# A hybrid two-layer diffusion step: row sums for 28 adaLN pieces, one SSD matrix a head, and products of zeros in the prologue

## The chip, the cores and the metric

The kernel runs on one core of one Trainium2 chip. The metric is the device time of one execution in microseconds. The engines that matter here are TensorE (PE, matmuls, and PEld, its weight loads), VectorE (DVE), ScalarE (ACT), GpSimd (POOL) and SyncE (SP, which issues nearly all DMAs).

## What is computed

One inference step through two trunk layers of width 1024 for 640 tokens: 128 context tokens, conditioned by `c_ctx`, and 512 latent tokens, conditioned by `c`. Each layer has an adaLN projection, a combined input projection that feeds four mixers (a bidirectional Mamba-2 SSD, an S5, a differential attention and a windowed attention), an output projection, and a squared-ReLU MLP of width 4096. The change touches two of these computations. The first is the adaLN projection, from which the six parts (shift, scale and gate of the norm and of the MLP) come; a part has 1024 outputs for each of the two conditions:

```python
def adaln(cvec, w, b):
    m = jax.nn.silu(cvec) @ w + b                  # w: 1024 x 6144, a matrix a layer
    return jnp.split(m[:, None, :], 6, axis=-1)
...
    sh1, sc1, g1, sh2, sc2, g2 = adaln(cmod, P['w_mod'][l], P['b_mod'][l])
```

The second is the part of the SSD inside a chunk of 128 tokens, for 8 heads of 64 columns, forward and backward:

```python
def ssd_chunked_scan(x, dt, a_log, bm, cm, s0):
...
    lmat = jnp.exp(jnp.where(lower, seg, NEG_INF))
    xdt = xc * dtc[..., None]
    scores = jnp.einsum('bcthn,bcshn->bctsh', cc, bc) * lmat
    y_diag = jnp.einsum('bctsh,bcshp->bcthp', scores, xdt)
...
    y_f, s_f = ssd_chunked_scan(xs, dt[:, :, 0], a_log[0], bm, cm, s0[:, 0])
    y_b, s_b = ssd_chunked_scan(flip(xs), flip(dt[:, :, 1]), a_log[1], flip(bm), flip(cm), s0[:, 1])
    y = y_f + flip(y_b) + d_skip.astype(f32)[:, None] * xs.astype(f32)
```

## The kernel before, in words

**Dense products.** Activations lie with features on partitions and the 640 tokens along the free axis, in two halves of 320. Every dense product splits both operands into a high and a low part: ACT copies the high part out (wh, L212), DVE or POOL subtracts it from the raw weights for the low part (wl, L196), and TensorE does three matmuls for each block of 128 rows: hi x hi (L223), lo activation x hi weights (L224) and hi activation x lo weights (L225). A half of a dense product with 1024 inputs is thus 24 matmuls of 128x320, and it ends in the PSUM tile dn, which has two buffers. An eviction on DVE or ACT frees it.

**The MLP** runs in four quarters. In each, eight products with w_fc1 (their evictions: ACT's ReLU, then DVE's product r at L1746, ACT's copy fh and the low part fl) are followed by eight with w_fc2, whose evictions are the residual adds on DVE (x, L1538, two instructions each, since context and latent tokens have gates of their own).

**adaLN pieces.** A piece is 256 outputs of one part. `adaln` multiplies the two conditions, padded to 32 columns (cpad), with eight blocks of w_mod (L288, eight matmuls in the code, 16 rows of the trace), copies the result to SBUF on ACT (mrow, L293), turns it with two matmuls by sel (L295, 4 rows of the trace), and adds the bias on DVE (mod, L298). Of 48 pieces in a layer, the prologue does parts 0 and 1 of layer 0 (`panel_adaln`, weights in wm); the other 40 come from `adaln_ahead`, with weights in the ring wa, which has eight buffers of 128x512. Of layer 0's other 16, four run in the mixers' stage, eight in the output projection, and the four of part 5 in the MLP. The 24 of layer 1 run in layer 0's MLP, too. There the function `between` is called after every dense product and takes five steps in eight calls out of one list: pieces, then the steps of the S5 build of layer 1 (`s5_build`, which prepares the S5's matrices on DVE, POOL, ACT and, at L633 and L660, TensorE), then pieces again.

**SSD.** For each of five chunks a layer and two groups of four heads: ACT makes the exponentials ee of both directions (tile sseg), POOL multiplies them by the masked scores of the backward direction into mf (L1033), DVE multiplies them in place by those of the forward direction (L1034), and TensorE then does two matmuls a head, one for each direction, with x times dt (sxd, two products on POOL at L1006): L1037 and L1038, 80 of each over the ten chunks of the two layers, each 128x64 and two rows of the trace. The masked scores themselves (scb) come from DVE at L999.

**Prologue.** TensorE's first work are the pieces of parts 0 and 1 in four panels q, whose weights (wm, 1 MB for each part and panel) come by DMA; beside them ACT and DVE square x for the first norm, and TensorE sums the squares into rb.

**What sets the order.** The instructions of each engine run in a fixed order that a scheduler writes down at build time from its own estimates; `tc.high_priority` moves a block ahead in it, and `tc.issue_after` places one behind a given instruction. Semaphores hold an instruction until its inputs and buffers are there.

## Time and profile before

| what | value |
|---|---|
| median of 3 runs | 2989.94 us (2985.88 to 3001.45) |
| the profiled execution: time, span of its trace | 2994.21 us, 2992.4 us |
| busy: PE, DVE, ACT, POOL | 95%, 56%, 39%, 28% of the span |
| mean granted TensorE clock | 0.976 |
| stretches: prologue, mixers of layer 0, output projection and norm, MLP of layer 0 | to 62, to 960, to 1062, to 1605 us |
| mixers of layer 1, MLP of layer 1 | to 2430, from 2515 us |

The page gives the busy time of each engine, the span in slices, the DMA queues, and the chain of work that ended last, followed back from the end. The trace behind it can be asked for groups of instructions by line, for waits (which engine stood still, at which line, and who released it), for windows of time, and for the plain sequence of an engine. A busy time on TensorE is the length of records that lap over each other, since matmuls are pipelined; the start-to-start distance tells what a row holds up.

### The profile page before, as it was taken

How to read it: one execution, taken by the hardware profiler on the slowest of the kernel's cores; microseconds unless marked ns; L12 is line 12 of the kernel's file. 1: busy time of each engine (PE TensorE's matmuls, PEld its weight loads, DVE VectorE, ACT ScalarE, POOL GpSimd, SP SyncE). 2: the span in 40 equal slices, each digit the busy share in tenths (PEclk: the TensorE clock that was granted, in tenths of full speed). 3: DMA queues.
4: the chain of work that ended last, by engine and by line, in shares of the span. 5: the costliest groups of instructions: out<-in, count | busy, mean ns of one | idle time of the engine just before them, and what ended most of it. 6: DMA issues, size and time to landing. Idle time of an engine off the chain costs nothing.

```text
span 2992.4 us, 53739 instructions
## 1 busy us (share of the span) xinstructions
PE 2831.8 (95%) x20782; PEld 2651.5 (89%) x20782; DVE 1686.3 (56%) x3574; ACT 1181.3 (39%) x2692; POOL 832.8 (28%) x823
## 2 busy tenths in 40 slices
PE   7889998999799999999999999989999999999999
PEld 5878988898689888899998989978997999999999
DVE  7859737665543456646235686576665436433333
ACT  4344563253344242323234555424534434332322
POOL 2743106522212222424111220363131131211111
PEclk9989999998899999999999999989999999999999
DMA  6753343234432635434443433432262323222222
GB/s 225 256 174 112 100 136 102 80 99 136 141 100 75 239 103 174 146 114 159 153 144 112 158 100 115 136 92 66 86 198 86 103 89 106 68 75 78 75 75 85
DMA packets 241855, 364.19 MB, mean 122 GB/s; under 512 B 42272, under 2 KB 104480, under 8 KB 241600
## 3 DMA queue, kind: packets, MB, share of 16 engines
q1 hardware_dynamic: 226848, 336.97, 36.0%
q10 hardware_dynamic: 14752, 23.78, 2.2%
q8 instruction: 164, 2.69, 0.4%
q14 instruction: 91, 0.75, 0.1%
HBM read 294.98 MB, written 65.68 MB: 121 GB/s over the span
## 4 chain that ended last, share of the span: by engine, by line
PE 72%; DVE 13%; DMA 4%; issue 3%; ACT 2%; POOL 2%; SPq 0%; DVEq 0%; ACTq 0%; POOLq 0%
PE dn L223 20%; PE dn L224 20%; PE dn L225 20%; DVE wl L196 2%; DMA sseg<-acum 1%; PE mx L288 1%; PE mx L1278 1%; PE pb L1322 1%; PE mx L1407 1%; PE mx L1452 1%; PE mx L1316 1%; DVE B L767 1%; DVE sc L766 1%; PE mx L743 1%; DVE cv L902 1%
## 5 line engine op out<-in xcount | busy, mean ns | idle before, releaser
L196 POOL TENSOR_TENSOR wl<-wr,wh 128x512 fp32r<-128x512 f32 x207 | 287.1, 1387 | 1340.7 <-ACT wh L212 1254.5
L212 ACT CAST wh<-wr 128x512 fp32r<-128x512 f32 (+1 forms) x614 | 377.3, 620 | 600.5 <-PE dn L224 525.1
L196 DVE TENSOR_TENSOR wl<-wr,wh 128x512 fp32r<-128x512 f32 (+1 forms) x407 | 326.4, 805 | 318.1 <-ACT wh L212 306.4
L223 PE MATMUL dn<-hh,wh 128*128 128x320 f32 x1328 | 422.3, 318 | 12.3 <-ACT us L695 3.8
L224 PE MATMUL dn<-hl,wh 128*128 128x320 f32 x1328 | 420.2, 316 | 2.8 <-DVE hl L401 1.5
L225 PE MATMUL dn<-hh,wl 128*128 128x320 f32 x1328 | 418.8, 316 | 1.6 <-DVE wl L196 1.6
L223 PE MATMUL dn<-nh,wh 128*128 128x320 f32 x992 | 311.1, 314 | 6.6 <-DVE r L1746 6.6
L223 PE MATMUL dn<-fh,wh 128*128 128x320 f32 x1008 | 313.6, 311 | 2.9 <-DVE x L1538 2.9
L224 PE MATMUL dn<-nl,wh 128*128 128x320 f32 x992 | 308.5, 311 | 3.9 <-DVE nl L401 1.6
L225 PE MATMUL dn<-fh,wl 128*128 128x320 f32 x1008 | 312.1, 310 | 0.0
L224 PE MATMUL dn<-fl,wh 128*128 128x320 f32 x1008 | 311.8, 309 | 0.0
L225 PE MATMUL dn<-nh,wl 128*128 128x320 f32 x992 | 307.6, 310 | 0.0
L223 PEld LDWEIGHTS dn<-hh,wh 128*128 128x128 f32 x1328 | 253.4, 191 | 19.4 <-ACT us L695 4.1
L223 PE MATMUL dn<-wh,hh 128*128 128x256 f32 (+1 forms) x880 | 259.2, 296 | 8.2 <-DVE dtraw L1207 3.0
L224 PE MATMUL dn<-wl,hh 128*128 128x256 f32 (+1 forms) x880 | 256.8, 293 | 10.5 <-DVE wl L196 8.5
L224 PEld LDWEIGHTS dn<-hl,wh 128*128 128x128 f32 x1328 | 253.3, 191 | 8.3 <-issue 3.2
L225 PEld LDWEIGHTS dn<-hh,wl 128*128 128x128 f32 x1328 | 253.2, 191 | 6.9 <-issue 3.8
L225 PE MATMUL dn<-wh,hl 128*128 128x256 f32 (+1 forms) x880 | 256.0, 292 | 0.0
L1538 DVE SCALAR_TENSOR_TENSOR x<-dn,mod,x 128x192 f32<-128x192 f32 (+2 forms) x240 | 98.0, 436 | 225.2 <-PE dn L225 217.7
L223 PE MATMUL dn<-B,wh 128*128 128x320 f32 x640 | 206.2, 323 | 12.7 <-ACT B L825 3.4
L224 PE MATMUL dn<-B,wh 128*128 128x320 f32 x640 | 202.1, 316 | 0.2 <-DVE B L196 0.2
L225 PE MATMUL dn<-B,wl 128*128 128x320 f32 x640 | 200.4, 313 | 0.0
(399 smaller groups left out, 6505.6 us busy)
## 6 DMA issues: line engine op xcount, KB each, us to landing
wr<-in_w_fc_dram SPq DMA_DIRECT2D x256, 256.0 KB, 2.8
wa<-in_w_mod_dram SPq DMA_DIRECT2D x160, 256.0 KB, 4.5
wr<-in_w_gate_dram SPq DMA_DIRECT2D x128, 256.0 KB, 2.8
wr<-in_w_tok_dram SPq DMA_DIRECT2D x80, 256.0 KB, 2.9
wr<-in_w_branch_dram SPq DMA_DIRECT2D x64, 256.0 KB, 3.0
acc<-gth SPq DMA_DIRECT2D x48, 320.0 KB, 3.1
gold<-acc SPq DMA_DIRECT2D x48, 320.0 KB, 3.7
gate<-gah ACTq DMA_DIRECT2D x70, 160.0 KB, 1.8
```

Of the source, the lines that this page charges most:

```text
L196: engine.tensor_tensor(out=out, in0=full, in1=hi, op=ALU.subtract)
L212: nc.scalar.copy(out=hi, in_=raw)
L223: nc.tensor.matmul(ps, sh, vh, start=first, stop=False)
L224: nc.tensor.matmul(ps, sh, vl, start=False, stop=False)
L225: nc.tensor.matmul(ps, sl, vh, start=False, stop=last)
L288: nc.tensor.matmul(acc[r0:r0 + 32, i * 256:i * 256 + 256], cpad[:, k, :], raw(part, k // 2)[:, c0:c0 + 256], start=(n_ < 4), stop=(n_ >= 4),)
L743: nc.tensor.matmul(xs[:, ri, g * NI:(g + 1) * NI], pm[:, ri, g * 128:(g + 1) * 128], U[:, g0 + g], start=True, stop=True)
L766: nc.vector.tensor_tensor(out=t, in0=v.to_broadcast(shp), in1=x.to_broadcast(shp), op=ALU.mult)
L767: nc.vector.tensor_tensor(out=dst, in0=dst, in1=t, op=ALU.add)
L902: nc.vector.scalar_tensor_tensor(out=cv, in0=xp[:, k:k + 646], scalar=cw[:, f, k:k + 1], in1=cv, op0=ALU.mult, op1=ALU.add)
L1278: nc.tensor.matmul(sc[:, n, c0:c0 + (k1 - k0) * 128], qT[rows[n], g, ct], kT[rows[n], k0:k1].rearrange("p k c -> p (k c)"), start=True, st ...
L1538: nc.vector.scalar_tensor_tensor(out=xs, in0=ps[:, c0:c1], scalar=mods[l][:, part * 8 + f, s:s + 1], in1=xs, op0=ALU.mult, op1=ALU.add)
```

## The change

There are three edits.

**Row sums.** Part 5 of both layers and parts 0 to 4 of layer 1 are no longer computed on TensorE. Of the pieces before, 28 go: the four of part 5 of layer 0 and the 24 of layer 1. In their place `adaln_rows` loads, for each block of 128 outputs, the 128x1024 block of the transposed weights (a new input, w_modt), and lets DVE multiply it with a condition that is the same on all partitions and sum along the row, with the bias as start (`tensor_tensor_reduce`, two for each block, one for each condition; each is two rows in the order, both at L352). The conditions come through DRAM: silu on a new input c_rows in the prologue, stored to c_d, and broadcast to 128 partitions in each MLP (`cond_rows`, 1 MB). 96 row sums run in layer 0's MLP and 16 (its own part 5) in layer 1's. `fill` places one behind each residual add and each product r. The ring wa has three buffers of 128x1024 now, `between` takes one step of the S5 build in every sixth call, and the build's tiles s5u and s5v have one buffer each in the MLP.

**SSD.** The two directions' masked scores are scaled by dt (a column for each row of the matrix, so it can stand on either side of the product) and added before the exponentials come in: ACT's scaled copy and DVE's scalar-tensor-tensor for each head, tile smd. DVE multiplies ee by the sum, and one matmul a head with x itself (L1075) remains. POOL's products mf and sxd for this sum are gone.

**Zeros.** `busy(n)` multiplies a tile of zeros in bf16, 128x128 by 128x128, n times: 80 times at the start, 120 times behind the first panel's adaLN, 40 times behind the second's call.

```diff
-    t1=3, tx=4, tq=6, ty=2, tw=5, td=5, nt=4, wa=8, wr=4, wh=4, wl=4, fh=10,
+    t1=3, tx=4, tq=6, ty=2, tw=5, td=5, nt=4, wa=3, wr=4, wh=4, wl=4, fh=10,
...
+    cr = tmp([128, 16], "cr", bufs=1)
+    sp.dma_start(out=cr, in_=a["c_rows"])
...
+    nc.vector.tensor_tensor(out=cr, in0=cr, in1=crt, op=ALU.mult)
+    c_d = dp.tile([128, 16], F32, name="c_d")
+    sp.dma_start(out=c_d, in_=cr)
...
+                    if n // 2 not in halves:
+                        halves[n // 2] = wa([128, 1024], "wa")
+                        sp.dma_start(out=halves[n // 2], in_=a["w_mod"][part * 4 + q, n // 2])
...
+    def cond_rows():
+
+        cb = big([128, 2, D], "cb")
+        sp.dma_start(out=cb.rearrange("p s k -> p (s k)"), in_=c_d.rearrange("a b -> (a b)").unsqueeze(0).to_broadcast((128, 2 * D)))
+        return cb
+
+    def adaln_rows(l, parts, cb, after=()):
+
+        for part in parts:
+            for f in range(part * 8, part * 8 + 8):
+                with tc.high_priority(offset=AHEAD):
+                    w = wa([128, D], "wa")
+                    sp.dma_start(out=w, in_=a["w_modt"][l * 48 + f - 40])
+                prod = mx().rearrange("p a b -> p (a b)")
+                for s in range(2):
+                    nc.vector.tensor_tensor_reduce(
+                        out=prod, in0=w, in1=cb()[:, s], scale=1.0, scalar=bmod[l][:, f:f + 1], op0=ALU.mult,
+                        op1=ALU.add, accum_out=mods[l][:, f, s:s + 1],
+                    )
+                    if s and f % 8 == 7 and part in after:
+                        make_gsc(l, after[part])
+                    yield
...
-            u, v = big(shape, "s5u", bufs=2, where=where), big(shape, "s5v", bufs=2, where=where)
+            u, v = (big(shape, t, bufs=2 if where == "build" else 1, where=where) for t in ("s5u", "s5v"))
...
-            xd = [times(dt[:, c, 8 * d:8 * d + 8], "sxd") for d in range(2)]
...
+                md = tx([128, 4, 128], "smd")
+                for h in range(4):
+                    n = 4 * g + h
+                    nc.scalar.activation(out=md[:, h], in_=cm[:, 0, g], func=AF.Copy, scale=dt[:, c, n:n + 1])
+                    nc.vector.scalar_tensor_tensor(
+                        out=md[:, h], in0=cm[:, 1, g], scalar=dt[:, c, 8 + n:9 + n], in1=md[:, h], op0=ALU.mult,
+                        op1=ALU.add,
+                    )
...
-                eng("mf").tensor_tensor(out=mf, in0=ee, in1=cm[:, 1, g].unsqueeze(1).to_broadcast(b4), op=ALU.mult)
-                eng("ef").tensor_tensor(out=ee, in0=ee, in1=cm[:, 0, g].unsqueeze(1).to_broadcast(b4), op=ALU.mult)
+                nc.vector.tensor_tensor(out=ee, in0=ee, in1=md, op=ALU.mult)
...
-                    nc.tensor.matmul(yp[:, hc], ee[:, h], xd[0][:, hc], start=True, stop=False)
-                    nc.tensor.matmul(yp[:, hc], mf[:, h], xd[1][:, hc], start=False, stop=True)
+                    nc.tensor.matmul(yp[:, hc], ee[:, h], r["xs"][:, c, hc], start=True, stop=True)
...
+        def busy(n):
+            for _ in range(n):
+                nc.tensor.matmul(rb[:, 1, 384:512], idle, idle, start=True, stop=True)
+
+        busy(80)
...
+                busy((120, 40, 0, 0)[q])
...
-        adgen = adaln_ahead(0, range(2, 6), {4: 1})
+        adgen = adaln_ahead(0, (2, 3, 4), {4: 1})
...
+            def fill(ins):
+
+                with tc.issue_after(ins.ins):
+                    step(rows)
+
             def res(part, squares, f, hf, ps):
-                residual(l, part, ps, hf, f, x)
+                ins = residual(l, part, ps, hf, f, x)
...
+            cb = cond_rows()
+            step(adgen, 99)
+            rows, bgen = adaln_rows(l, (5,), lambda: cb), iter(())
...
+                rows = itertools.chain(rows, adaln_rows(l + 1, range(5), lambda: cb, {1: 0, 4: 1}))
+                bgen = s5_build(l + 1, "mlp", lambda: act0[7][1][0:1, 0, T - 1:T].bitcast(F32))
...
-                step(bgen, turn * 5 // 8 - (turn - 1) * 5 // 8)
+                step(bgen, int(turn % 6 == 0))
```

TensorE in layer 0's MLP, the end of one half of a product with w_fc2 (fh and fl are the activations), before:

```order
L225 MATMUL dn_15993<-fh_15061,wl_15963 128x320
L223 MATMUL dn_15993<-fh_15063,wh_15962 128x320
L288 MATMUL mx_16179<-wa_16177,cpad 32x256 x2
L288 MATMUL mx_16179<-wa_16175,cpad 32x256 x2
L288 MATMUL mx_16179<-wa_16173,cpad 32x256 x2
L288 MATMUL mx_16179<-wa_16171,cpad 32x256 x2
L288 MATMUL mx_16331<-wa_16329,cpad 32x256 x2
L288 MATMUL mx_16331<-wa_16327,cpad 32x256 x2
L288 MATMUL mx_16331<-wa_16325,cpad 32x256 x2
L288 MATMUL mx_16331<-wa_16323,cpad 32x256 x2
L224 MATMUL dn_15993<-fl_15064,wh_15962 128x320
L225 MATMUL dn_15993<-fh_15063,wl_15963 128x320
```

and after, the same product:

```order
L223 MATMUL dn_15831<-fh_14990,wh_15796 128x320
L224 MATMUL dn_15831<-fl_14991,wh_15796 128x320
L225 MATMUL dn_15831<-fh_14990,wl_15797 128x320
L223 MATMUL dn_15831<-fh_14992,wh_15796 128x320
L224 MATMUL dn_15831<-fl_14993,wh_15796 128x320
L225 MATMUL dn_15831<-fh_14992,wl_15797 128x320
```

The rows of L288, which stood between the three matmuls of one block, are gone, and the 24 matmuls of a half follow each other.

DVE in layer 0's MLP (r and x are evictions of dn, wl and fl low parts), before:

```order
L1746 TENSOR_TENSOR r_2342_12275<-r_2342_12275,dn_12250 128x320
L196 TENSOR_TENSOR fl_11879<-r_2342_12275,fh_11878 128x320
L1746 TENSOR_TENSOR r_2350_12317<-r_2350_12317,dn_12292 128x320
L196 TENSOR_TENSOR fl_11881<-r_2350_12317,fh_11880 128x320
L196 TENSOR_TENSOR wl_12449<-wr_12446,wh_12448 128x512
L196 TENSOR_TENSOR wl_12455<-wr_12452,wh_12454 128x512
L1746 TENSOR_TENSOR r_2352_12347<-r_2352_12347,dn_12322 128x320
L196 TENSOR_TENSOR fl_11881<-r_2352_12347,fh_11880 128x320
L298 TENSOR_TENSOR mod_93<-mx_12360,bmod_89 128x4
```

and after, further on, where the build's steps (L528, L530) begin:

```order
L1802 TENSOR_TENSOR r_2371_12811<-r_2371_12811,dn_12786 128x320
L352 ISA mx_12784,mod_101<-wa_12782,cb_12429,bmod_97 128x1024
L352 ISA mod_101 128x1
L196 TENSOR_TENSOR fl_12109<-r_2371_12811,fh_12108 128x320
L1575 SCALAR_TENSOR_TENSOR x_11311<-dn_12829,mod_101,x_11311 128x128
L1575 SCALAR_TENSOR_TENSOR x_11311<-dn_12829,mod_101,x_11311 128x192
L352 ISA mx_12858,mod_101<-wa_12856,cb_12429,bmod_97 128x1024
L352 ISA mod_101 128x1
L528 TENSOR_TENSOR s_zr_12897<-s5prm_12890,s_step_12895 128x32
L196 TENSOR_TENSOR wl_13099<-wr_13096,wh_13098 128x512
L530 TENSOR_TENSOR s_zi_12899<-s5prm_12890,s_step_12895 128x32
```

A row sum, two rows at L352, stands directly behind each eviction of dn, ahead of the low part of that eviction's result or of the next weights; the add of L298 is gone.

TensorE in the SSD stage of layer 0, four heads of one chunk, before:

```order
L225 MATMUL dn_5737<-B_5186,wl_5700 128x320
L1037 MATMUL mx_4505<-sxd_4501,sseg_4507 128x64
L1038 MATMUL mx_4505<-sxd_4503,sseg_4508 128x64
L1037 MATMUL mx_4505<-sxd_4501,sseg_4507 128x64
L1038 MATMUL mx_4505<-sxd_4503,sseg_4508 128x64
L1037 MATMUL mx_4505<-sxd_4501,sseg_4507 128x64
L1038 MATMUL mx_4505<-sxd_4503,sseg_4508 128x64
L1037 MATMUL mx_4505<-sxd_4501,sseg_4507 128x64
L1038 MATMUL mx_4505<-sxd_4503,sseg_4508 128x64
L223 MATMUL dn_5736<-B_5186,wh_5693 128x320
```

and after:

```order
L225 MATMUL dn_5990<-B_5440,wl_5948 128x320
L1075 MATMUL mx_4735<-xs_3624,sseg_4746 128x64 x4
L223 MATMUL dn_6059<-hh_118,wh_6049 128x320
L224 MATMUL dn_6059<-hl_119,wh_6049 128x320
L225 MATMUL dn_6059<-hh_118,wl_6050 128x320
```

Of eight rows that took turns between the two directions (sseg and sxd in two versions), four are left, with xs as the moving operand.

## Rows read from the trace of the kernel before

**Rows 1.** The page: busy time by engine, and the last chain by engine.

```profile
PE 2831.8 (95%) x20782; PEld 2651.5 (89%) x20782; DVE 1686.3 (56%) x3574; ACT 1181.3 (39%) x2692; POOL 832.8 (28%) x823
...
PE 72%; DVE 13%; DMA 4%; issue 3%; ACT 2%; POOL 2%; SPq 0%; DVEq 0%; ACTq 0%; POOLq 0%
```

**Rows 2.** Windows: us, PE busy (rows), PEld, DVE, ACT, POOL, PE clock, DMA, GB/s.

```profile
1100.00:1600.00 500.00, 489.30 (x3788) 455.44 (x3787) 249.75 (x517) 145.34 (x298) 135.36 (x123) 1.00 0.45 144
1350.00:1400.00 50.00, 47.04 (x442) 45.45 (x440) 41.82 (x70) 19.40 (x42) 25.35 (x24) 1.00 0.50 167
2550.00:2950.00 400.00, 398.61 (x2718) 398.35 (x2717) 134.93 (x260) 124.04 (x241) 68.69 (x61) 1.00 0.25 77
450.00:540.00 90.00, 79.66 (x543) 71.45 (x542) 68.68 (x111) 29.29 (x75) 60.62 (x48) 0.96 0.37 105
```

**Rows 3.** Waits of PE (us, times, longest): from 1070 to 1605, then to 60.

```profile
PE dn L223 <- DVE r L1746: 7.2, 7, 1.4
PE dn L223 <- DVE x L1538: 2.9, 2, 2.2
...
PE mx L288 <- DMA wm<-in_w_mod_dram: 13.6, 4, 7.6
```

**Rows 4.** PE's groups by line, 1062 to 1605: busy, mean ns | idle before, releaser.

```profile
L288 PE MATMUL mx<-wa,cpad 128*32 128x256 f32 x432 | 33.1, 384 | 2.8 <-DMA wa<-in_w_mod_dram 2.8
L660 PE MATMUL pb<-s5qt,s5bz 128*32 128x112 f32 x256 | 14.6, 264 | 0.0
L295 PE MATMUL mx<-sel,mrow 128*128 128x2 f32 x112 | 14.1, 234 | 0.0
L633 PE MATMUL pb<-ident,s5pt 128*128 128x128 f32 x64 | 11.6, 276 | 0.0
```

**Rows 5.** PE's sequence at 1591: start, us, engine, line, operation, number of rows.

```profile
1591.17 0.95 PE L295 MATMUL mx<-sel,mrow 128*128 128x2 f32 x8
1591.98 0.39 PE L223 MATMUL dn<-fh,wh 128*128 128x320 f32 x1
1592.21 0.31 PE L224 MATMUL dn<-fl,wh 128*128 128x320 f32 x1
```

**Rows 6.** DVE's groups by line, the whole span, shapes kept apart.

```profile
L196 DVE TENSOR_TENSOR wl<-wr,wh 128x512 fp32r<-128x512 f32 x403 | 322.9, 805 | 317.2 <-ACT wh L212 305.5 <-PE dn L225 5.3 <-DMA pm<-s5p 3.8
...
L902 DVE SCALAR_TENSOR_TENSOR cv<-xp,cw,cv 128x646 f32<-128x646 f32 x72 | 68.2, 948 | 1.8
...
L1440 DVE SCALAR_TENSOR_TENSOR dp<-dp,drc,dp 128x640 f32<-128x640 f32 x32 | 29.5, 922 | 0.6
...
L1291 DVE TENSOR_REDUCE wm<-mx 128x2 f32<-128x1024 f32 x16 | 19.6, 1225 | 41.2 <-PE mx L1285 41.1
```

**Rows 7.** PE's sequence in the SSD stage.

```profile
464.43 0.39 PE L1038 MATMUL mx<-sxd,sseg 128*128 128x64 f32 x2
464.65 0.39 PE L1037 MATMUL mx<-sxd,sseg 128*128 128x64 f32 x2
464.87 0.39 PE L1038 MATMUL mx<-sxd,sseg 128*128 128x64 f32 x2
```

**Rows 8.** Groups by line from 445 to 545, layer 0's SSD: DVE, POOL, PE.

```profile
L1034 DVE TENSOR_TENSOR sseg<-sseg,scb 128x512 f32<-128x512 f32 x10 | 11.2, 1121 | 0.3
...
L999 DVE TENSOR_TENSOR scb<-pa,triu 128x128 f32<-128x128 f32 x10 | 2.8, 281 | 0.5 <-PE mx L1038 0.4
...
L1041 DVE TENSOR_TENSOR xs<-mx,sxD 128x512 f32<-128x512 f32 x4 | 2.7, 683 | 2.0 <-POOL sxD L1006 2.0
...
L1033 POOL TENSOR_TENSOR sseg<-sseg,scb 128x512 f32<-128x512 f32 x10 | 14.3, 1430 | 9.2 <-ACT sseg L1027 6.7 <-ACT dcl L1021 1.4 <-DMA gate<-gah 1.1
...
L1037 PE MATMUL mx<-sxd,sseg 128*128 128x64 f32 x74 | 14.6, 280 | 4.5 <-DVE sseg L1034 4.5
```

**Rows 9.** PE's sequence: the first pieces, one at 38, bf16 rows at 833.

```profile
9.29 1.08 PE L288 MATMUL mx<-wm,cpad 128*32 128x256 f32 x8 [0.27 <-DMA wm<-in_w_mod_dram]
...
38.21 2.79 PE L288 MATMUL mx<-wm,cpad 128*32 128x256 f32 x24
...
833.42 0.40 PE L1285 MATMUL mx<-maskb,identb 128*128 128x128 bf16 x4
```

**Rows 10.** DVE's sequence in the prologue: two short forms.

```profile
42.73 0.14 DVE L1347 TENSOR_SCALAR dgs<-dgs 128x1 f32<-128x1 f32 x1
...
46.00 0.22 DVE L298 TENSOR_TENSOR mod<-mx,bmod 128x4 f32<-128x4 f32 x2
```

More of the change, by code (lines that the diff above doesn't have):

```diff
@@ L277, in hybrid_body @@
     nc.vector.tensor_tensor(out=cpad[:, :, 0:2], in0=cs, in1=csg, op=ALU.mult)
+    cr = tmp([128, 16], "cr", bufs=1)
+    sp.dma_start(out=cr, in_=a["c_rows"])
+    crt = tmp([128, 16], "crt", bufs=1)
+    nc.scalar.activation(out=crt, in_=cr, func=AF.Tanh, scale=0.5)
+    nc.vector.tensor_scalar(out=crt, in0=crt, scalar1=0.5, scalar2=0.5, op0=ALU.mult, op1=ALU.add)
+    nc.vector.tensor_tensor(out=cr, in0=cr, in1=crt, op=ALU.mult)
+    c_d = dp.tile([128, 16], F32, name="c_d")
+    sp.dma_start(out=c_d, in_=cr)
     def adaln(l, parts, q, acc, out, raw, ks=range(KT)):
@@ L311, in raw @@
                 def raw(part, n, q=q, halves=halves):
-                    if n not in halves:
-                        halves[n] = wa([128, 512], "wa")
-                        sp.dma_start(
-                            out=halves[n], in_=a["w_mod"][l, part * 4 + q, n // 2][:, (n % 2) * 512:(n % 2) * 512 + 512]
-                        )
-                    return halves[n]
+                    if n // 2 not in halves:
+                        halves[n // 2] = wa([128, 1024], "wa")
+                        sp.dma_start(out=halves[n // 2], in_=a["w_mod"][part * 4 + q, n // 2])
+                    return halves[n // 2][:, (n % 2) * 512:(n % 2) * 512 + 512]
                 for n in range(KT // 2):
@@ L1537, in residual @@
             xs = x[:, f, hf * HF + c0:hf * HF + c1]
-            nc.vector.scalar_tensor_tensor(
+            ins = nc.vector.scalar_tensor_tensor(
                 out=xs, in0=ps[:, c0:c1], scalar=mods[l][:, part * 8 + f, s:s + 1], in1=xs, op0=ALU.mult, op1=ALU.add
             )
+        return ins
     def h_tiles(name):
@@ L1566, in hybrid_body @@
         accs, rb = mx(), mx()
+        idle = cp.tile([128, 128], BF16, tag="idle", name="idle")
+        nc.vector.memset(idle, 0.0)
+        def busy(n):
+            for _ in range(n):
+                nc.tensor.matmul(rb[:, 1, 384:512], idle, idle, start=True, stop=True)
+        busy(80)
         us = [big([128, 8, NI], "us0", bufs=2) for _ in range(2)]
@@ L1575, in panel_adaln @@
                 for i in range(2):
-                    sp.dma_start(out=w[part][i], in_=a["w_mod"][0, part * 4 + q, i])
+                    sp.dma_start(out=w[part][i], in_=a["w_mod"][part * 4 + q, i])
             if soon:
@@ L1720, in hybrid_body @@
             acc_n = big([128, T], "acc_n")
+            rows = iter(())
+            def fill(ins):
+                with tc.issue_after(ins.ins):
+                    step(rows)
             def res(part, squares, f, hf, ps):
-                residual(l, part, ps, hf, f, x)
+                ins = residual(l, part, ps, hf, f, x)
                 if squares:
                     square_into(acc_n, x, f, hf)
+                fill(ins)
             for f in range(KT - NTAIL):
@@ L1745, in squares @@
                 nc.scalar.activation(out=r, in_=ps, func=AF.Relu)
-                nc.vector.tensor_tensor(out=r, in0=r, in1=ps, op=ALU.mult)
+                ins = nc.vector.tensor_tensor(out=r, in0=r, in1=ps, op=ALU.mult)
                 hi, lo = hsl(act[j], 0, hf)
@@ L1749, in squares @@
                 sub_lo(lo, r, hi)
+                fill(ins)
             act0 = []
@@ L1793, in hybrid_body @@
             step(bgen, 99)
+            step(rows, 99)
             if l + 1 < L:
@@ L1846, in _pack @@
     p["c_t"] = np.stack([_col(inp["c_ctx"]), _col(inp["c"][0])], -1)
+    p["c_rows"] = np.stack([inp["c_ctx"], inp["c"][0]]).reshape(128, 16)
+    w = inp["w_mod"][0].reshape(2, 4, 128, 24, 256)
     p["w_mod"] = st([
-        st([
-            w.reshape(2, 4, 128, 24, 256)[s, :, :, q].transpose(1, 0, 2).reshape(128, 1024) for q in range(24) for s in range(2)
-        ]).reshape(24, 2, 128, 1024) for w in inp["w_mod"]
-    ])
+        w[s, :, :, q].transpose(1, 0, 2).reshape(128, 1024) for q in range(20) for s in range(2)
+    ]).reshape(20, 2, 128, 1024)
+    p["w_modt"] = np.concatenate([inp["w_mod"][0].T.reshape(48, 128, D)[40:], inp["w_mod"][1].T.reshape(48, 128, D)])
     p["b_mod"] = _col(inp["b_mod"])
```

11 lines of the change are left out of this document (2 added, 9 removed).

## The prediction

> **What bounds the kernel now.** I read the page first [rows 1]: TensorE is busy 95% of the span and carries 72% of the chain that ended last, DVE 13%. So what leaves TensorE shortens the program, as long as nothing takes its place there; where DVE or a DMA ends the wait, a cut on TensorE is worth less. The change touches three stages, so I took each apart.
>
> The MLP of layer 0 (1062 to 1605 us) holds all 28 pieces that go. I compared its window with one of layer 1's MLP, which has neither pieces nor an S5 build [rows 2]: there TensorE is busy 398.6 of 400 us and DVE 134.9, 0.337 of the time. In layer 0 TensorE has 489.3 of 500 and DVE 249.8; the short window shows DVE at 41.8 of 50 while build steps run. The waits of that stretch [rows 3] say who was late then: TensorE waited 7.2 us for r and 2.9 us for x, both of them DVE's evictions of dn. So DVE already costs 10 us here, in bursts.
>
> **Pieces on TensorE, removed.** In the stretch the matmuls of L288 are busy 33.1 us for 432 rows, 27 pieces of 16, and those of L295 14.1 us for 112 rows, 28 pieces of 4 [rows 4]. For 28 pieces: 33.1 x 28/27 + 14.1 = 48.4 us. Busy time laps over the neighbours, so I looked at one visit [rows 5]: eight rows of L295 take 0.95 us, the next dn starts 0.81 us after the first of them and its successor 0.23 later, where the pace is 0.147 (398.6 us by 2718 rows in layer 1 [rows 2]). 0.81 + 0.08 is 0.89, 0.94 of the busy time. 48.4 x 0.94 = 45.5, and 2.8 us of waits for wa [rows 4] go as well: **-48 us**. The 28 copies on ACT and the adds on DVE (0.11 us each [rows 10]) were hidden. The DMA volume stays: 28 pieces of two 512 KB blocks before, 56 blocks after, and two broadcasts of 1 MB. The 12 pieces that stay in layer 0 have three buffers of 4 KB a partition in place of eight of 2 KB: 0 to +3 us (the size of the waits for wa now); I take 0.
>
> **Row sums on DVE, added.** Two for each of 56 blocks, 112: 96 in layer 0's MLP, 16 in layer 1's. No row shows one. A reduction over 1024 elements reads 1225 ns [rows 6]; a two-input row over 512 reads 683 ns [rows 8], so 1024 would be that and 512 elements at one per cycle, the same 1.2 us. The instruction that writes the sum is at least the 0.14 us of the smallest DVE rows [rows 10]. Lower bound 1.37 us. POOL works beside it, and such rows then stretch: 1121 ns for 512 elements in the SSD stage against 683 [rows 8], a factor of 1.64. If POOL were there all along, 2.01 + 0.14 = 2.15 us, the upper bound. The rows of wl, which share this stage, average 805 against 683, 1.18 [rows 6]; by them I take 1.225 x 1.18 + 0.14 = 1.59.
>
> The order puts one row sum behind each eviction of dn, 24 matmuls or 3.53 us apart. In the first ten gaps and the last twenty DVE has slack: 1.19 (0.337 of 3.53) + 1.59 = 2.78. In some 66 gaps between, the build runs too, now one step in six turns. There TensorE has 66 x 3.53 = 233 us plus 26 of the build's own matmuls (L633, L660) [rows 4], 259. DVE has 0.337 x 259 = 87, the build's 78 (249.8 - 0.337 x 500 - 3 for the adds) and 66 x 1.59 = 105: 270. **It is full**, 270 against 259. What is queued behind a row sum on DVE is the next eviction and the lo half of the next weights; dn has two buffers, so TensorE waits once an eviction is some 3 us late. With the old 10 us of waiting and no more the net is 0 (the lower bound: at 1.37 us the sum is 255, under 259, and the build is spread thinner); at 2.15 us DVE has 307, so 48 of waiting and +38. I take 22 us of waiting, **+12 net**, 11 for the overload and as much for bursts. The build's products have one buffer in place of two, so POOL's next product waits for DVE; the new order puts other work between, and the cost is in these 12. The row sums hardly wait themselves: by the order on SP a block is loaded four gaps (14 us) ahead. In layer 1's MLP 16 of them fall on a DVE at a third: 0.
>
> [...]
>
> **One SSD matrix a head.** L1038 goes, 160 rows. At full pace two of them hold their neighbours apart by 0.22 us [rows 7], so 80 x 0.22 = **-18 us**. The two factors of the matrix now meet on DVE: eight scalar-tensor-tensors a chunk, 80 in all, at about the 281 ns of a 128x128 row [rows 8], 22 us on a DVE that is busy 69 of 90 us [rows 2]; ACT's 80 scaled copies fall on an engine at 29 of 90. Against it, POOL loses the mf products (1430 ns [rows 8]) and as many and as large scaled x, 20 of each, 55 us for both layers. POOL beside it is why DVE's rows take 1121 instead of 683 ns; of 60 such rows up to 0.44 us each comes back, 26 us. And the DVE product wrote over what POOL's product still read, so it came after it; that 1.4 us a group leaves the path. TensorE waited 4.5 us for these products in layer 0 [rows 8], part of which goes: -2. Bounds: 0 if DVE's added 22 us end up on the path, -32 if its waits in both layers go too. I take **-20**.
>
> **Prologue.** [...] Four bf16 rows at 833 us take 0.40 us [rows 9], 0.10 each; allow 0.06 to 0.12, then 80 take 5 to 10 us, 120 take 7 to 14, 40 take 2.4 to 5. [...] **-2**, bounds -6 and +6.
>
> **Sum:** -48 + 12 - 20 - 2 = -58. The profiled execution took 2994.2 us (span 2992.4), the median is 2989.9; on the median that gives 2932.
>
> **The rivals.** *DVE full.* The row sums take the 2.15 us of the upper bound: +38 in place of +12, so -32, 2958. For it: DVE is full at my own price already; against it, POOL is idle two thirds of the time. *SSD set by DVE.* The 18 us on TensorE turn into waits for sseg: -38, 2952. For it: DVE at 69 of 90 and TensorE already waiting; against it, POOL loses half of its work. [...] *The change doesn't do what it says:* zeros don't raise the clock and hold TensorE up; that is +8 on the forecast, inside its range.
>
> **How the numbers follow.** Forecast 2932, its own range 2900 to 2950, chance 0.57. DVE full 0.15 (0.05 of it within 0.5%), SSD set by DVE 0.13, two passes 0.15 (0.06 within, 0.09 slower). The range leaves out the two passes and the ends of the rest: 2898 (no cost on DVE -12, SSD at -32, prologue at -6 give 2904, and some for the new order) to 2972 (DVE full and SSD set by DVE give 2978, seldom together). A measurement of this kernel tells about 0.5%, 15 us, from no change: faster 0.57 + 0.10 + 0.13 = 0.80, same 0.11, slower 0.09.
>
> **What would show it.** In the profile after: row sums of 1.4 to 1.7 us, DVE near 95% in the middle of layer 0's MLP with TensorE's waits there for r and x at 15 to 30 us, and that MLP some 36 us shorter. Row sums above 2.4 us would make the prediction wrong. In the SSD stage TensorE's rows halve, the product on DVE falls from 1.1 towards 0.8 us, and the waits for it shrink. In the prologue L288 runs at the full clock well before 38 us.

## The result and the profile after

| | before | changed |
|---|---|---|
| median | 2991.69 us | 2956.14 us (2946.63 to 2957.13) |
| ratio | 1 | 0.9871, 95% interval 0.9837 to 0.9904 |
| span of the profiled execution | 2992.4 us | 2955.3 us |
| mean granted TensorE clock | 0.976 | 0.965 |

The change saves 36 us by the medians, 39 by the ratio, 29 to 49 by its interval. The forecast was 58 saved, with a range of 2898 to 2972 us: the time is inside the range and 24 us above the forecast. The parts behind the sum missed in both directions.

The two mean clocks count different things at the start: the record of the granted clock begins with its first rise, at 41.7 us before and at 6.4 us with the zeros, and what lies ahead of it counts as full (eight rows of a piece take 1.08 us there in the kernel before [rows 9], and 0.61 in its layer 0's MLP [rows 4]). From 62 us on the means are 0.976 and 0.968.

The busy times by engine, from the page of the changed kernel, answer to [rows 1]:

```profile
PE 2791.6 (94%) x20302; PEld 2641.8 (89%) x20302; DVE 1828.7 (62%) x3853; ACT 1195.6 (40%) x2745; POOL 800.8 (27%) x783
```

TensorE lost 40 us of busy time and DVE gained 142. The windows (columns as in [rows 2]) of the changed kernel: the stretch of layer 0's MLP in which row sums and S5 build run together, the end of that MLP, and layer 0's SSD stage:

```profile
1130.00:1390.00 260.00, 238.40 (x1813) 228.85 (x1812) 248.96 (x442) 69.23 (x142) 109.79 (x91) 0.97 0.51 165
1490.00:1560.00 70.00, 70.00 (x479) 70.00 (x478) 30.19 (x58) 24.64 (x48) 10.99 (x9) 1.00 0.34 107
...
460.00:550.00 90.00, 80.25 (x529) 70.94 (x531) 83.39 (x176) 41.65 (x114) 47.59 (x40) 0.94 0.39 112
```

In the first, DVE is busy 249 of 260 us, TensorE 238, and the granted clock is 0.97, where the kernel before had 1.00 in its whole MLP window. In the second DVE is at 0.43: all row sums are over by then.

To see where the time goes I matched the products of the two traces (the k-th matmul of each form with the k-th) and read how much earlier or later each stands in the changed kernel. One product is read near each place; in the dense stages its neighbours agree to about 1 us, around the norms and the SSD they differ by up to 7:

| place in the kernel before | later (+) or earlier (-) | what lies between |
|---|---|---|
| 41 us, first dense product | +4.5 | prologue |
| 250 us | +10.7 | start of layer 0's mixers |
| 700 us | -9.8 | layer 0's SSD, 445 to 575 |
| 1050 us | -10.6 | the rest of the mixers, output projection |
| 1590 us | -35.5 | layer 0's MLP |
| 1920 us | -31.1 | start of layer 1's mixers |
| 2039 us | -48.3 | layer 1's SSD |
| 2440 us | -43.8 | rest of layer 1's mixers |
| 2480 us | -38.2 | layer 1's output projection |
| end | -36.8 | layer 1's MLP |

Layer 0's MLP gave 25 us, not 36; the two SSD stages gave some 17 us each (at 445 us the changed kernel is 9 us late, at 575 it is 8 early), more than 20 together; it was 7 us late at the end of the prologue (62 us) and 8 to 11 at 250 us; and some 11 us went in layer 1's second half.

### The profile page after: what moved, and what is told of

Same layout as the page of the kernel before. It is cut to its first block, busy times and chain, and to the rows that moved or that the text cites. A ratio compares the mean times of both kernels' runs of the same rounds, so it can differ in the third digit from the quotient of the medians.

```text
span 2955.3 us, 52897 instructions
## 1 busy us (share of the span) xinstructions
PE 2791.6 (94%) x20302; PEld 2641.8 (89%) x20302; DVE 1828.7 (62%) x3853; ACT 1195.6 (40%) x2745; POOL 800.8 (27%) x783
## 4 chain that ended last, share of the span: by engine, by line
PE 46%; DVE 6%; DMA 2%; ACT 1%; issue 1%; POOL 1%; SPq 0%; ACTq 0%; POOLq 0%; DVEq 0%
PE dn L223 14%; PE dn L224 13%; PE dn L225 13%; DMA sseg<-acum 1%; DVE wl L196 1%; PE mx L1444 1%; PE mx L1315 1%; PE pb L1359 1%; PE mx L1353 1%; PE mx L1489 0%; DVE s5u L624 0%; DVE mx L352 0%; DVE smd L1053 0%; DVE qks L1215 0%; PE mx L774 0%
## 5 line engine op out<-in xcount | busy, mean ns | idle before, releaser
L196 POOL TENSOR_TENSOR wl<-wr,wh 128x512 fp32r<-128x512 f32 x207 | 295.1, 1426 | 1305.0 <-ACT wh L212 1226.9
L196 DVE TENSOR_TENSOR wl<-wr,wh 128x512 fp32r<-128x512 f32 (+1 forms) x407 | 317.9, 784 | 269.6 <-ACT wh L212 263.5
L223 PEld LDWEIGHTS dn<-nh,wh 128*128 128x128 f32 x992 | 189.5, 191 | 15.4 <-DVE r L1802 12.5
```

What stands on the lines that cost most here:

```text
L196: engine.tensor_tensor(out=out, in0=full, in1=hi, op=ALU.subtract)
L223: nc.tensor.matmul(ps, sh, vh, start=first, stop=False)
```

## The experiments

The prediction's terms are theory A in what follows, the reading of the table above is theory B. All ratios are against the kernel before, run beside each kernel on the same chip; the four sets of experiments ran on four chips (2997 to 2999 us for the kernel before), so kernels of two sets are compared by their ratios.

**Each part alone.** Four kernels: the changed one without `busy`, and the kernel before with one part of the change each.

```diff
# no_zeros: the changed kernel
-        busy(80)
...
-                busy((120, 40, 0, 0)[q])
# zeros_only, ssd_only, rows_only: the kernel before
+ those calls of busy; or the new lines of ssd_core; or all the rest of the change
```

> The changed kernel without its three rows of zero products in the prologue; row sums and SSD stay. Theory A (the prediction's terms): the zeros gave 2 us, so 2956 becomes 2958. Theory B (the traces of before and after, matched product by product): at 80 us the changed kernel is 11 us late, and 8 of them last to the SSD stage; the zeros held TensorE, so 2956 becomes about 2948.

> The kernel before with the zero products alone. Theory A: 2 us faster than before, 2988. Theory B: 8 us slower, 2998.

> The kernel before with the one SSD matrix a head alone. Theory A: 20 us faster, 2970. Theory B: matched products move by 18 us across layer 0's SSD stage and by 11 across layer 1's, so 29 faster, 2961.

> The kernel before with the row sums alone (28 pieces off TensorE, their weights loaded as rows). Theory A: 36 us faster, 2954. Theory B: 25 won in layer 0's MLP and up to 8 lost again at the end of layer 1's mixers, where row weights are loaded ahead of x, so 17 to 25 faster, 2965 to 2973.

| kernel | ratio (95%) | us against before (2998) | prediction's term |
|---|---|---|---|
| zeros alone | 1.0026 (1.0011 to 1.0041) | +8 (+3 to +12) | -2 |
| one SSD matrix alone | 0.9904 (0.9890 to 0.9919) | -29 (-33 to -24) | -20 |
| row sums alone | 0.9950 (0.9929 to 0.9972) | -15 (-21 to -8) | -36 |
| all but the zeros | 0.9820 (0.9804 to 0.9837) | -54 (-59 to -49) | -56 |

Theory B holds for the zeros and the SSD. For the row sums both theories were too high (36, and 17 to 25), though the interval reaches to 21. Without the zeros the kernel is at 2944.6 us.

The three parts alone add up to -36, what the whole change gives by the medians, but that sum is luck in part, since the parts don't simply add. Beside the SSD edit the row sums gave 25 us (2969.6 to 2944.6; 19 to 32 by the two intervals) where alone they gave 15, and in the changed kernel the zeros cost 15 us (0.9871 against 0.9820; 4 to 26) where alone they cost 8. Both differences are at the edge of what these intervals can tell.

**What the row sums cost.** The sums are left out, so the six parts are a constant, while all their loads stay.

```diff
+            nc.vector.memset(mods[l][:, part * 8:part * 8 + 8], 0.5)
...
-                    nc.vector.tensor_tensor_reduce(
...
```

> The changed kernel without zeros, with the 112 row sums left out: their weights and the broadcasts are loaded as before, but the six parts that they make are a constant. It prices DVE's work alone, against the kernel without zeros (ratio 0.982 to before, 54 us faster). Theory A (the prediction): TensorE's waits for DVE in layer 0's MLP fall from 22 to some 10 us, so 12 us more, ratio 0.978. Theory B (trace of after): the waits for r, x, s5pt and s5qt in layer 0's MLP are 22 us and each also costs stretches of half clock, so 15 to 20 us more, ratio 0.976.

Measured: 0.9754 (0.9735 to 0.9773), 20 us less than with the row sums (0.9820; the difference is known to about 8 us). Theory B, by the time. Next to the 24.9 us that layer 0's MLP gained, this makes the pieces worth some 45 us, close to the 48 of the prediction; the matched products agree, by which layer 0's MLP of the kernel without row sums is 46 us shorter than before. The waits of TensorE in layer 0's MLP (us in total, times, longest), first in the changed kernel, from 1058 to 1570:

```profile
PE dn L223 <- DVE r L1802: 12.9, 9, 2.8
PE dn L223 <- DVE x L1575: 4.9, 5, 1.3
PE pb L664 <- DVE s5pt L626: 3.9, 5, 1.6
PE pb L691 <- DVE s5qt L626: 1.1, 1, 1.1
```

and with the row sums left out, from 1058 to 1545:

```profile
PE dn L223 <- DVE r L1789: 5.7, 5, 1.5
PE dn L223 <- DVE x L1571: 1.4, 3, 0.6
PE dn L223 <- DVE mod L346: 1.3, 1, 1.3
...
```

Against 10 us before [rows 3], 22.8 us are waits for DVE now. When the row sums go, 7 us for r and x stay, and all waits in that MLP fall from 23 to 9 us (the kernel without zeros has 23, too). The other half of theory B, that each wait costs a stretch of lower clock as well, doesn't hold. The build's stretch with the row sums (the kernel without zeros) and without them:

```profile
1115.00:1375.00 260.00, 238.15 (x1836) 229.00 (x1835) 250.48 (x452) 69.49 (x143) 108.83 (x91) 0.99 0.52 167
1130.00:1390.00 260.00, 252.47 (x1902) 240.33 (x1901) 175.80 (x315) 73.94 (x148) 104.59 (x94) 0.99 0.34 112
```

DVE falls from 250 to 176 us, and the granted clock is 0.99 in both; over the whole of that MLP the clock stands at its lower level (0.50 granted) for 13.0 us with the row sums and 13.5 without. So of the 18 us that this MLP gains without them (509.5 to 491.6 us) 14 are waits, and none is clock.

The longest wait shows how they come about. DVE's sequence in the changed kernel around 1188 us (start, us, engine, line, operation):

```profile
1182.51 0.48 DVE L1802 TENSOR_TENSOR r<-r,dn 128x320 f32<-128x320 f32 x1
1182.90 1.74 DVE L352 CUSTOM_DVE_ANT_0 mx<-wa,cb,bmod 128x1024 f32<-128x1024 f32 x1
...
1184.57 1.36 DVE L626 TENSOR_TENSOR s5qt<-s5u,s5v 128x512 f32<-128x512 f32 x1
1185.96 1.67 DVE L624 TENSOR_TENSOR s5u<-s5pou,s5nc 128x512 f32<-128x512 f32 x1
1187.55 1.58 DVE L196 TENSOR_TENSOR wl<-wr,wh 128x512 fp32r<-128x512 f32 x1
1189.06 0.47 DVE L1802 TENSOR_TENSOR r<-r,dn 128x320 f32<-128x320 f32 x1
1189.45 1.28 DVE L352 CUSTOM_DVE_ANT_0 mx<-wa,cb,bmod 128x1024 f32<-128x1024 f32 x1
```

and what TensorE does meanwhile:

```profile
1189.58 0.41 PE L223 MATMUL dn<-nh,wh 128*128 128x320 f32 x1 [2.77 <-DVE r L1802]
```

Between two evictions (r at 1182.51 and at 1189.06) DVE does a row sum, two rows of the build and one of the weights, each drawn out to 1.4 to 1.7 us beside POOL (with no POOL row beside it a row sum takes 1.28 us in this kernel, and wl 0.69 in the kernel before). The second eviction, which frees dn, takes 0.47 us; TensorE stood for 2.77. The row sum's 1.74 us are less than that, so it did not do this by itself: it pushed the queue further back.

**Where the row sums stand.** One variant (on the kernel without zeros, with the late loads below) lays the 96 row sums out by DVE's load; a second one gives the build's tiles back their second buffer and takes one of wa's three for it.

```diff
-                    step(rows)
+                    step(rows, share(l, next(gaps)))   # 1; 3 of 5 while the build runs; then 1, 2, 1, 2
...
-            u, v = (big(shape, t, bufs=2 if where == "build" else 1, where=where) for t in ("s5u", "s5v"))
+            u, v = (big(shape, t, bufs=2, where=where) for t in ("s5u", "s5v"))   # second variant, with wa=2
```

> The changed kernel without zeros, with late loads in layer 1 and the same 96 row sums in layer 0's MLP laid out by DVE's load: one behind each eviction for the first 24, three for every five evictions while the S5 build runs (72 evictions), three for every two in the last 20, where DVE was at 0.3 to 0.5. Theory A (DVE's total is what is full: 270 us of work against 259 in the build's stretch; with 30 row sums fewer there it has 50 us less): half or more of the 20 us that the row sums cost comes back, ratio 0.977 to 0.978. Theory B (the waits come from single bursts: a build step and a row sum between two evictions, whatever the average): 5 us or less, ratio 0.980.

> The run with the row sums laid out by load (ratio 0.9795), with two buffers each for the build's tiles s5u and s5v in layer 0's MLP, as the kernel before had; two buffers of wa instead of three pay for the space. Theory A (the waits for r come from row sums and build steps that meet, not from the single buffers): TensorE's waits for r and s5pt stay at 15 us, ratio 0.979 to 0.980, or worse if two buffers of wa make row sums wait for their weights. Theory B (with one buffer DVE stands behind POOL's product of the last step, and the evictions behind it): the waits fall by half, ratio 0.977.

Measured: 0.9795 (0.9768 to 0.9822) and 0.9799 (0.9783 to 0.9816). The first is 4 us under the kernel with late loads (0.9810), less than the intervals can tell, and its own interval holds the forecasts of both theories. The waits have to decide. The windows of the first, the build's stretch and the end of the MLP:

```profile
1130.00:1390.00 260.00, 244.13 (x1774) 226.73 (x1773) 216.43 (x384) 68.49 (x139) 105.56 (x91) 0.97 0.45 145
1480.00:1540.00 60.00, 60.00 (x411) 60.00 (x410) 55.70 (x97) 21.78 (x44) 11.60 (x8) 1.00 0.62 202
```

DVE went from 249 to 216 of 260 us, and its work moved to the end, where TensorE stays at 60 of 60 beside a DVE at 0.93. Yet the waits for r were 11.4 us in 11 places (14.6 in 10 with the late loads alone), all waits of TensorE in that MLP 17.3 us (23.7), and the clock stayed at 0.97. With DVE far from full most of the waiting is still there, which speaks for theory B: a burst between two evictions costs more than the average. The second buffer changed nothing that can be measured in the time (waits for r 12.4 us; those for s5pt are gone, those for x are 3.4).

**Loads ahead of x.** In layer 1 the first three row weights are issued ahead of x for the output projection. SP's queue in the changed kernel:

```profile
2427.16 1.37 SPq L349 DMA_DIRECT2D wa<-in_w_modt_dram  x3
2430.84 0.82 SPq L200 DMA_DIRECT2D wr<-in_w_out_dram  x1
2431.70 3.50 SPq L1785 DMA_DIRECT2D x<-x_d  x6
```

DVE's residual waits for x:

```profile
2437.83 1.13 DVE L1575 SCALAR_TENSOR_TENSOR x<-dn,mod,x 128x128 f32<-128x128 f32 x3 [1.71 <-DMA x<-x_d]
```

and TensorE for DVE:

```profile
2438.65 0.38 PE L223 MATMUL dn<-mh,wh 128*128 128x320 f32 x1 [3.77 <-DVE x L1575]
```

```diff
-                with tc.high_priority(offset=AHEAD):
+                with tc.high_priority(offset=late_by):   # 400 instead of 2000 in layer 1
```

> The changed kernel without zeros, with the first row weights of layer 1's MLP issued on SP behind the eight loads of x instead of ahead of them. Theory A (the prediction, which gave these loads no price): no change against the kernel without zeros, ratio 0.982. Theory B (the matched products lose 5 us at the start of layer 1's output projection, where DVE waits for x): 5 us more, ratio 0.980, and the wait of TensorE for x there gone.

Measured: 0.9810 (0.9796 to 0.9825) against 0.9820 (0.9804 to 0.9837). The interval holds both theories. TensorE's wait for x there (2.2 us in the kernel without zeros) is gone from the trace, and the matched products of the output projection gain 4 us on that kernel, which they had lost elsewhere (at 230 us, ahead of the edit); in the time the edit cannot be told from nothing. The other traces say the same of the wait: it is 3.8 us in the changed kernel, 3.2 with the row sums alone and 3.8 with them left out, which all have the early loads, and it is in neither the kernel before nor the one with the SSD edit alone.

**What the SSD edit lives on.** The prediction said 18 us from TensorE's rows. Two kernels make one matrix a head and keep POOL's work as dead work (its result is read by nothing): in the first mf and sxd are still made; in the second mf's substitute reads the scaled scores, so that DVE's product over ee need not come after it.

```diff
+                nc.gpsimd.tensor_tensor(out=mf, in0=ee, in1=cm[:, 1, g].unsqueeze(1).to_broadcast(b4), op=ALU.mult)
                 nc.vector.tensor_tensor(out=ee, in0=ee, in1=md, op=ALU.mult)
...
+            xd = [...]   # both products x times dt on POOL, read by nothing
# second kernel: out=dead, in0=md in place of out=mf, in0=ee
```

> The kernel before with one SSD matrix a head, but with POOL's products mf and sxd still made, as dead work. Theory A (the prediction: 18 us come from TensorE's rows, 2 from the waits): it stays at about 18 to 20 us faster than before, ratio 0.9935. Theory B (most of the extra 9 us come from POOL leaving DVE alone): 20 us faster than before or less, against the 29 of the SSD edit alone, ratio 0.993 to 0.997. Theory C (POOL's relief is worth nothing): as the SSD edit alone, ratio 0.990.

> The kernel before with one SSD matrix a head, and with as much dead work on POOL as in the run that kept mf and sxd (ratio 1.000), but the product that took mf's place reads the scaled scores instead of the exponentials, so DVE's product over the exponentials no longer comes after it. Theory C (the wait of DVE's product for POOL's product is what ate the gain): most of the 29 us of the SSD edit is back, ratio 0.991 to 0.993. Theory D (POOL's time is what counts: DVE's rows stretch beside it, and its other products, which the stage needs, queue behind the dead ones): ratio 0.996 to 1.000.

Measured: 1.0001 (0.9988 to 1.0015) and 0.9983 (0.9970 to 0.9996), against 0.9904 without the dead work. The first lies outside all three theories, the second inside theory D. With POOL's products kept, the edit loses 29 us, and 24 when DVE's product needn't wait for them: it then gains next to nothing, though TensorE has 160 rows less. Busy times by engine, with the SSD edit alone, with POOL's work kept, and with its substitute beside (before: [rows 1]):

```profile
PE 2806.3 (95%) x20622; PEld 2630.8 (89%) x20622; DVE 1687.4 (57%) x3654; ACT 1206.1 (41%) x2772; POOL 783.8 (26%) x783
PE 2820.6 (94%) x20622; PEld 2645.5 (88%) x20622; DVE 1714.8 (57%) x3654; ACT 1204.8 (40%) x2772; POOL 832.1 (28%) x823
PE 2819.7 (94%) x20622; PEld 2644.1 (88%) x20622; DVE 1701.5 (57%) x3654; ACT 1206.0 (40%) x2772; POOL 841.2 (28%) x823
```

With the edit alone POOL loses 49 us and DVE stays where it was (1686.3 before), in spite of its new rows; with POOL's work kept DVE has 27 and 14 us more. TensorE's group of the one matmul a head in layer 0 (busy, mean ns | idle before, releaser), with the SSD edit alone and with POOL's work kept:

```profile
L1044 PE MATMUL mx<-xs,sseg 128*128 128x64 f32 x80 | 11.2, 287 | 8.6 <-DVE sseg L1041 8.6
```

```profile
L1049 PE MATMUL mx<-xs,sseg 128*128 128x64 f32 x80 | 11.5, 291 | 10.3 <-DVE sseg L1046 10.3
```

TensorE waits longer for this product in both than before (4.5 us [rows 8]). All its waits in the two SSD stages add up to 12.5 and 15.6 us before, 13.9 and 13.9 with the edit alone, 18.9 and 24.5 with POOL's work kept, and 18.3 and 25.8 with the substitute. In the first kernel the waits for the product (sseg) make the difference, 26.5 us over the run against 13.4 with the edit alone; in the second they are 12.7, and the rest is waits for other work of ACT and DVE. Theory C of the second run, that the wait for POOL's product alone eats the gain, falls. Two things stay untested: taking POOL's work away without the new matrix, and the room of the dead tiles (sxd and the substitute stand in the ring tx, which has four buffers and holds scb and smd, too). The new work on DVE is dearer than I had it, in the changed kernel (ns min/median/max):

```profile
L1053 DVE SCALAR_TENSOR_TENSOR smd<-scb,dtd,smd x80: 334/343/1382, 458.4 to 1964.7; 128x128 f32<-128x128 f32 x80
```

With the SSD edit alone, the 48 of the 80 with no POOL row beside them average 345 ns, the other 32 take 791, together 42 us and not 22. They fit because POOL's relief gives DVE as much back (1687.4 us busy over the run against 1686.3 before).

**Which zeros cost.** Two kernels leave some of them out.

```diff
-                busy((120, 40, 0, 0)[q])
+                busy((120, 0, 0, 0)[q])     # zeros_first; zeros_80 has busy(80) alone
```

> The changed kernel with the first 80 and the 120 zero products, without the last 40. Theory Z1: the 40 stand directly ahead of the last pieces and the first dense product, at half clock (4.45 us), and hold DVE's norm up through the tile that both use, so nearly all of the loss goes: 2944 to 2948, ratio 0.983. Theory Z2: the 120 hold the pieces of the later panels up, so it stays at the changed kernel's 2956, ratio 0.987.

> The changed kernel with only the first 80 zero products, which end before the first weights are there (8.26 us). Theory Z3 (the loss is the 40 and the 120, which stand in TensorE's queue ahead of pieces): as the kernel without zeros, ratio 0.982. Theory Z4 (any zeros at the start bring the later half-clock stretches with them): as with the first 200, ratio 0.985.

Measured: 0.9851 (0.9830 to 0.9873) and 0.9835 (0.9818 to 0.9851), between none (0.9820) and all (0.9871). Each step is within the intervals of its neighbours, so the times don't say which zeros cost how much, only that all of them together do. The matched products say it for the prologue: at 62 us the kernel without zeros is 1.9 us late, with the first 80 it is 1.2, with the 120 as well 4.5, and with all of them 7.2. What the zeros do is seen in TensorE's sequence of the changed kernel:

```profile
1.29 7.03 PE L1611 MATMUL mx<-idle 128*128 128x128 bf16 x80 [1.29 <-DVE idle L1607]
8.26 2.13 PE L298 MATMUL mx<-wm,cpad 128*32 128x256 f32 x32
...
13.80 8.17 PE L1611 MATMUL mx<-idle 128*128 128x128 bf16 x120 [1.66 <-DVE mod L308]
22.04 0.64 PE L298 MATMUL mx<-wm,cpad 128*32 128x256 f32 x8
...
26.98 1.08 PE L298 MATMUL mx<-wm,cpad 128*32 128x256 f32 x8 [0.61 <-DMA wm<-in_w_mod_dram]
...
38.95 4.45 PE L1611 MATMUL mx<-idle 128*128 128x128 bf16 x40
43.33 2.18 PE L298 MATMUL mx<-wm,cpad 128*32 128x256 f32 x32
45.45 0.41 PE L223 MATMUL dn<-hh,wh 128*128 128x320 f32 x1
```

They do raise the clock: 1.00 is granted from 6.4 us, where the record begins, to 13.2 and again from 16.6 to 26.8 us; 32 rows of a piece take 2.13 us at 8.26, and eight take 0.64 at 22.04, where eight took 1.08 before [rows 9]. But from 22 to 31 us TensorE waits for wm, DVE and again wm, and at 26.98 eight rows take 1.08 us: from 26.8 to 43.9 us the granted clock is 0.50. The last 40 products run in that stretch, 0.11 us each (0.07 for the 120), directly ahead of the last pieces and of the first dense product, which comes at 45.45 instead of 40.93. With 80 zeros alone TensorE then waits 10.4 us for wm, eight rows take 1.08 us at 22.28, and a dense row at 45.72 still takes 0.61, where the one at 45.45 above takes 0.41. Later, from 200 to 270 us, the granted clock is 0.85 in the changed kernel, where the kernel before and the one without zeros have 0.93 and 0.95. That isn't the zeros' doing. The same stretch in the changed kernel and in the one with late loads, which has no zeros:

```profile
200.00:270.00 70.00, 62.05 (x440) 60.53 (x439) 41.20 (x87) 35.65 (x76) 24.71 (x29) 0.85 0.47 145
200.00:270.00 70.00, 61.57 (x430) 59.74 (x429) 39.33 (x79) 36.45 (x74) 24.63 (x27) 0.85 0.42 135
```

Two more kernels without zeros (row sums left out, laid out by load) have 0.85 there, and the one with 80 zeros has 0.93. One trace of each kernel does not show what makes the difference.

## Why the prediction was right, and where its steps failed

- **What bounds the kernel.** Right: TensorE is at 94%, and the pieces that left it came off the time, less what TensorE now waits for DVE.
- **Pieces, -48.** Right within what can be told: 45 us by the times with the row sums left out, known to about 8, and 46 in the matched products. (A layer has 24 pieces; the 48 of which the prologue does 8 are those of both layers.)
- **One row sum, 1.59 us.** Right in size: in the changed kernel (ns min/median/max) it is

```profile
L352 DVE CUSTOM_DVE_ANT_0 mx<-wa,cb,bmod x112: 1271/1284/2270, 1085.7 to 2579.1; 128x1024 f32<-128x1024 f32 x112
L352 DVE DVE_READ_ACCUMULATOR2_ANT mod<- x112: 128/138/160, 1086.9 to 2580.3; 128x1 f32 x112
```

  with a mean of 1451 + 138 = 1589 ns. That the mean of wl was the right guide is luck in part: 63 of the 112 have no POOL row beside them and average 1283 ns, the other 49 average 1666. The "one per cycle" of the prediction is 1.05 ns an element by the rows of 128 and 512 elements (281 and 683 ns [rows 8]); no row shows how long a cycle is.
- **Two passes.** The prediction gives 0.15 to a row sum of two passes. No run shows one: a row sum over 1024 elements takes 1271 to 1306 ns where no POOL row stands beside it, less than two products over 512 (683 ns each [rows 8]) and near the one reduction over 1024 in the kernel before (1225 ns [rows 6]); two of those would be 2.45 us.
- **DVE full, +12.** The wait was right in sum: 22 us forecast, 22.8 seen, so the net of 12 came as forecast. How it was split is not borne out: half of it was put down to the overload, and with DVE at 216 of 260 us 17.3 of 23.7 us of waiting stayed. Leaving the row sums out is worth 20 us (12 to 27), 14 of them waits in this MLP, so their price lies at or above the 12. And layer 0's MLP became only 25 us shorter, not 36. What the sum left out is the clock: in this MLP it stands at its lower level, 0.50 granted, for 20.5 us in the changed kernel and for 3.4 before, some 8.5 us by an estimate that takes 0.50 for half the speed. The row sums don't cause it, as the run without them shows (13.5 us, and 13.0 in the kernel without zeros); what does stays open.
- **Row weights, "the DMA volume stays".** This step failed: the volume stays, but the loads moved ahead of x on SP. That is a wait of 2 to 4 us and 4 to 6 us in the matched products in four kernels that have it, though the run with the late loads could not show it in the time.
- **SSD, -20.** The direction was right, and the balance on DVE came out by luck. DVE's new rows were priced at 22 us and took 42; the relief of its 60 products of 128x512 was priced at up to 26 and was 10.6 (with the edit alone, they go from 64.1 to 53.5 us in the two stages). But DVE's other rows were relieved, too (those of swd from 17.5 to 10.3 us), and its busy time over the run stayed the same, 1686.3 and 1687.4 us. So the waits stayed as they were, 28.1 and 27.8 us in the two stages (the -2 did not come), and with the edit alone the stages became 23 us shorter in the matched products, near the 18 that were forecast for TensorE's rows. That is so only with POOL relieved, which the runs with dead work show and the sum did not have as a condition. Why the time fell by 29 us (24 to 33) and not by 20 is not shown. The rival, SSD set by DVE, was half right: waits for sseg rose from 7.4 to 14.4 us over the run, and still the stage became shorter.
- **Prologue, -2.** Wrong in sign: no run shows the 2 us. The zeros alone cost 8 (3 to 12), past the bound of +6 by its middle. They raised the clock, which was granted at 1.00 to 26.8 us with a gap of 3.4 us at 13.2, but it fell to 0.50 at the next waits for wm. And they take time of their own in TensorE's queue: the last 40 took 4.45 us, inside the 2.4 to 5 that I allowed, and stand directly ahead of the last pieces and the first dense product.

By the parts alone, the saving was forecast 21 us too high for the row sums, 10 too high for the zeros, and 9 too low for the SSD: 22 together, which is the 58 forecast less the 36 measured. By the order in which the parts were taken away it is 11 for the row sums (25 beside the SSD edit) and 17 for the zeros: 19 together, which is the 58 less the 39 of the ratio. The kernel without zeros, at -54, comes near its forecast of -56. That the total fell inside the range is luck in part: misses of both signs met in it. The bounds of the DVE term (to +38) had room for the miss of the row sums; those of the prologue had not for the middle of what the zeros cost.

The best by its ratio of the kernels that compute the whole step is the one with the row sums laid out by load, without zeros and with late loads: 2936.6 us, 0.9795. From the others of the whole change without zeros it can't be told apart (0.980 to 0.982). The changed kernel's interval (0.9837 to 0.9904) lies above its interval.

## What to carry to other kernels

Work that is moved to an engine with slack on average meets that engine's bursts: look for what stands ahead of the next eviction in its queue. Before charging a loss of clock to the new work, look at the same stretch in a kernel that leaves the work out; here the clock was lost there, too (13.5 us at 0.50 without the row sums). Before crediting a cut to the engine that was relieved most visibly, put the work of the other relieved engine back as dead work; here the gain was gone with it. The products of zeros raised the clock here, but it fell again at the next waits (0.50 granted from 26.8 to 43.9 us), and those that stood ahead of real work held it up.

## What the runs showed of the hardware

**A POOL row that reads held a DVE row of two SBUF inputs to its end.** On average, with the SSD edit alone, the scalar-tensor-tensor of 128 columns takes 345 ns with no POOL row beside it and 791 with one; in the changed kernel the row sum takes 1283 and 1666. A factor, as the prediction used, is the wrong form, and the averages hide the right one. In the changed kernel, POOL and then DVE:

```profile
1178.14 2.02 POOL L196 TENSOR_TENSOR wl<-wr,wh 128x512 fp32r<-128x512 f32 x1
1178.99 2.27 DVE L352 CUSTOM_DVE_ANT_0 mx<-wa,cb,bmod 128x1024 f32<-128x1024 f32 x1
```

POOL's row ends at 1180.16, 1.17 us after DVE's has begun, and DVE's ends 1.10 us later. The others are alike: of the 34 row sums that begin while a POOL row runs, the 29 that have more than 0.5 us of it ahead end 1085 to 1095 ns behind its end; the 15 that begin before a POOL row does take 1279 to 1286 ns, no more than alone. In the kernel before, of 66 rows of wl (128x512) that begin with more than 0.2 us of a POOL row ahead, 64 end 545 to 556 ns behind its end; the other two stand beside a memset of POOL, which reads nothing, and take 679 and 685 ns, no more than alone. Of the scalar-tensor-tensors that begin so, 19 of 20 end 146 to 151 ns behind it with the SSD edit alone, and all 16 end 145 to 154 ns behind it in the changed kernel. There the products r, which read dn in PSUM, lose nothing: the 26 that begin so take 484 ns on average, and those without a POOL row 483. What a DVE row of two SBUF inputs lost is thus the rest of the POOL row that it met, less 0.14 to 0.2 us, whatever its own length: up to 1.0 us in the row sums and 1.2 in wl.

**Two kinds of matmuls in turn.** In the changed kernel 32 rows of the build in one piece cost little; laid between dense rows two by two they are dear. TensorE's sequence at two places:

```profile
1194.55 0.97 PE L691 MATMUL pb<-s5qt,s5bz 128*32 128x112 f32 x32
1195.34 0.23 PE L697 MATMUL pb<-s5c,s5bz 128*32 128x16 f32 x8
...
1449.43 0.38 PE L691 MATMUL pb<-s5qt,s5bz 128*32 128x112 f32 x2
1449.74 0.41 PE L223 MATMUL dn<-fh,wh 128*128 128x320 f32 x1
1450.08 0.38 PE L691 MATMUL pb<-s5qt,s5bz 128*32 128x112 f32 x2
1450.39 0.41 PE L224 MATMUL dn<-fl,wh 128*128 128x320 f32 x1
```

In one piece 32 rows take 0.79 us to the next start, 0.05 for two. In turn, two of them and one dense row take 0.65, where 0.15 and 0.05 would be 0.20. This went on from 1449 to 1462 us with no wait in it, at the full granted clock. In layer 0's MLP a dense row is followed by a row of the build at 55 places before and at 64 in the changed kernel, so it is part of both times.
